# A hybrid attention layer on one core: head outputs stored as two half-precision parts and transposed by DMA on the way back

## The chip, the core and the metric

One core of a Trainium2 chip runs one launch of the kernel. Its engines have queues of their own, worked off in program order: TensorE (PE in the profile) multiplies matrices and also transposes, by a product with the identity; VectorE (DVE) and ScalarE (ACT) work element by element; GpSimd (POOL) and SyncE (SP) issue most of the DMA transfers here. The metric is the device time of a launch in microseconds (us), the median of several runs.

## What is computed

A decoder layer with two kinds of attention over one projected input, 2048 positions, width 1024, 16 heads of 64 columns, all in single precision:

```python
h = rms_norm(x, g_pre[l]) * (1.0 + scale[:, None, :]) + shift[:, None, :]
proj = h @ w_in[l]
qa, ka, va, fa, za, qb, kb, vb, zb = jnp.split(proj, split_points, axis=-1)
oa = forgetting_attention(qa, ka, va, fa + b_fgate[l])      # 8 heads, causal, reshapes left out
oa = oa * jax.nn.silu(za)
qb, kb = rope(qb, positions), rope(kb, positions)
ob = sliding_window_sink_attention(qb, kb, vb, sinks[l])    # 8 heads, window 128
ob = ob * jax.nn.silu(zb)
y = jnp.concatenate([oa, ob], axis=-1) @ w_out[l]
x = x + gate[:, None, :] * rms_norm(y, g_post[l])
```

The heads' outputs `oa` and `ob` side by side are the array of 2048 x 1024 that this change is about. It is multiplied by the gate `silu(z)` and then by `w_out`.

## The kernel before

Large products are made from half-precision parts: each single-precision operand is scaled and split into a high part and the rest (low), and high x high, high x low and low x high are summed in PSUM. That is why most products come in threes.

The kernel has four stages in one hand-written order. First come the adaLN projection and the normalised input. Then the sliding-window heads (`Pair`, 32 of them: four pairs of heads by eight pairs of 128-row blocks), with input projections as filler for TensorE between their steps. Then the forgetting heads (`Step`): 8 heads of 20 steps, each step two blocks of 128 keys against a chunk `ci` of 512 queries, again with projections as filler. Head 7 is the last; in it the weights `w_out` are loaded and split (`w_out_load`, `w_out_split`), and from its ninth step on the output projection is the filler (`ofill`). After the last step the rest of the output projection runs alone; this is the tail.

The order is written out by helpers. `after(n, f)` puts `f` off by `n` calls of `tick()`; a step of a head calls `tick` twice, the tail once every two filler units (`tick2`). A unit of the output projection (`ounits`) is the product of one slice of 128 rows for half the output columns: three matmuls (line 1489). A tile of 128 positions has 16 units.

A head's output goes this way. In `Step.pv` (line 1310) the last block of a chunk ends with a division by the row sum on VectorE (line 1327) into a tile `ona` of 128 x 256, which SP stores to DRAM, `o_d[ci]`, at line 1328; 32 such stores. In `Pair.pv` the same is done at line 913, and POOL stores at line 915; 32 stores. Rows of `o_d` are positions, so for the output projection, which needs the columns on the partitions, each tile of 128 positions must be transposed.

That is done by the class `Out`, one object for each of 16 tiles:

- `load` (line 1398) has SP load the tile's 128 x 1024 of `o_d` (line 1402, 512 KB) and its gate values `z_d` (line 1404, 512 KB) into slots of the array `Ts[0]`, which heads of even number use for their queries and keys. There are two slots of each, by the tile's parity.
- `turn` (line 1406) has TensorE make eight transposes of 128 x 128 in single precision into two PSUM banks (line 1410). Put off by ticks follow: the product with the gate on VectorE, two operations that read the banks (`gate`, line 1419); squares on ScalarE (1423); a matmul with ones that sums them over the partitions and the scale from it (1427, helper lines 121 and 122); the high part on ScalarE (1437) and the low part on VectorE (1438). The tile `oz` with both is what the products read.
- `product` (line 1476) makes the 16 units. Its evacuation reads PSUM on VectorE (1498) and ScalarE (1499); after the second half `root` and `store` follow, with `x` loaded at 1486 and the result stored at 1519, both by SP.

The loads of tiles 0 and 1 stand in head 7 behind its steps 4 and 6, their turns behind steps 6 and 8; tile 0's load needs chunk 0 of all heads in `o_d`, head 7's too. Later tiles are loaded at the first unit of the tile two before (`oloads`), and a turn is a unit of its own, behind the third unit of the tile before (line 1531). SP works its queue in order, so that a DMA whose input isn't there keeps all later ones waiting; in that part of head 7 the queue holds stores of outputs, loads of tiles, rows of query limbs (`ext_rows`, line 1208) and loads of `w_out` (line 1378).

Of the kernel before, what the change touches and what calls it, by code (L numbers as in the profile page):

```python
# [18 lines left out]
P = 128  # L19
# [22 lines left out]
def hybrid_layer(  # L42
# [33 lines left out]
    o_d = [dram.tile([CH, D], F32, name=f"o_d{t}") for t in range(NCH)]  # L76
# [189 lines left out]
    def w_split(key):  # L266
        w_scale(key)
        w_high(key)
        w_low(key, 0, 1)

# [566 lines left out]
    class Pair:  # L837
# [62 lines left out]
        def pv(self):  # L900
            j, i = self.j, self.i
            po = ps_pv.tile([P, 4, 64], F32, tag="pv", name="pob")
            for e, (i_, k0, nk) in enumerate(self.blocks):
                for h in range(2):
                    for b in range(nk):
                        for n, (pp_, vv) in enumerate(((0, 0), (0, 1), (1, 0))):
                            PE.matmul(po[:, 2 * e + h, :], self.ptt[:, pp_, self.at[e] + h * nk + b, :],  # L907
                                      vb[:, k0 + b, self.g, 64 * vv:64 * vv + 64],
                                      start=(b == 0 and n == 0), stop=(b == nk - 1 and n == 2))

            def out_():
                on = onp.tile([P, 2, P], F32, tag="on", name="on")
                V.tensor_tensor(on[:].rearrange("p e (h d) -> p (e h) d", h=2), po[:],
                                self.rinv[:].unsqueeze(2).broadcast_to([P, 4, 64]), op=ALU.mult)
                G.dma_start(o_d[i // 4][(i % 4) * P:(i % 4 + 2) * P, (4 + j) * P:(5 + j) * P]
                            .rearrange("(e p) c -> p e c", p=P), on[:])

            after(1, out_)
# [357 lines left out]
    class Step:  # L1276
# [33 lines left out]
        def pv(self):  # L1310
# [12 lines left out]
            if self.last:  # L1323
# [4 lines left out]
                SP.dma_start(o_d[self.ci][:, hd * 64:(hd + 1) * 64].rearrange("(u p) d -> p u d", p=P), on[:])  # L1328
# [26 lines left out]
    def open_out():  # L1355
        nonlocal op_, stp
# [4 lines left out]
        stp = foxo.enter_context(tc.tile_pool(name="stpo", bufs=4, reuse_waits="tile"))  # L1361
        oio["w"] = wo.tile([P, 2, KT, D], F16, name="wohl")
# [7 lines left out]
    w_raw = {}  # L1370
# [21 lines left out]
    class Out:  # L1392
# [5 lines left out]
        def load(self):  # L1398
            t = self.t
            rows_ = slice(t * P, (t + 1) * P)  # L1400
            self.o = Ts[0][:, t % 2, :].bitcast(F32)
            SP.dma_start(self.o, o_d[t // 4][(t % 4) * P:(t % 4 + 1) * P, :])
            self.z = Ts[0][:, 2 + t % 2, :].bitcast(F32).rearrange("p (k n) -> p k n", k=KT)
            SP.dma_start(self.z, z_d[:, :, rows_].rearrange("k p n -> p k n"))

        def turn(self, lag):

            px = [bk[bank()][:].rearrange("p (k n) -> p k n", k=4) for _ in range(2)]
            for k in range(KT):
                PE.transpose(px[k // 4][:, k % 4, :], self.o[:, k * P:(k + 1) * P], ident[:])  # L1410
# [5 lines left out]
            def gate():  # L1416
                for h in range(2):
                    z = self.z[:, 4 * h:4 * h + 4, :]
                    V.tensor_tensor(z, px[h], z, op=ALU.mult)
# [103 lines left out]
    ounits, oloads = [], {}  # L1523
    for t, n in [(0, 0), (1, 0), (0, 1), (1, 1)] + [(t, n) for t in range(2, NB) for n in range(2)]:
        if n == 0 and t + 2 < NB:
            oloads[len(ounits)] = t + 2
        for q in range(KT):
            ounits.append(lambda t=t, n=n, q=q: outs[t].product(n, q))
            nxt = 2 if (t, n) == (0, 1) else t + 1 if n == 0 and 2 <= t < NB - 1 else None
            if q == 2 and nxt:  # L1530
                ounits.append(lambda nxt=nxt: outs[nxt].turn(4))
    opos = [0]
    N_IN = 4 * KT + 1

    def ofill(n, each=None):
        for _ in range(n):
            if opos[0] in oloads:
                outs[oloads[opos[0]]].load()
# [5 lines left out]
    with tc.manual_schedule():  # L1544
# [99 lines left out]
        fxs.close()  # L1644
        ofill(len(ounits) - opos[0], tick2)
        for _ in range(4):
            tick()

    foxo.close()
# [32 lines left out]
```

## Time and profile before

| | us |
|---|---|
| runs: median (lowest, highest) of 3 | 1190.21 (1186.89, 1191.7) |
| span of the profiled execution | 1188.7 |
| TensorE matmuls busy | 1147.3 |
| VectorE busy | 914.1 |
| ScalarE busy | 665.9 |
| heads of forgetting attention end, tail begins | 1022.7 |
| last 48 matmuls begin | 1175.7 |

For the profiled execution the page gives its span, from the first to the last instruction, and no time beside it; the span lies 1.5 us under the median of the runs. Where the profile of a window is shown below, times are counted from the start of the span. In a timeline a row is the start, the duration, the engine, the line and the operation with the tile written and those read, `x` a count of instructions merged into the row, and in brackets the idle time before it with the instruction that ended it. In a table of groups the figures behind the bar are busy time in us and mean ns of one; behind the second bar stands the engine's idle time in front of them. TensorE's matmuls are pipelined, so a row of several lasts longer than the distance to the next one. `SPq` is the SP queue's issue of a DMA, not the transfer.

### The profile page before, as it was taken

The page shows a single profiled execution, that of the slowest core. Times are in us where ns is not written, and L with a number is a line of the kernel's source. Part 1 is how long each engine was busy: PE and PEld are TensorE (multiplying, and loading weights), DVE is VectorE, ACT ScalarE, POOL GpSimd, SP SyncE. Part 2 cuts the span into 40 slices and gives each one's busy share as a digit, 9 for nine tenths or more (in the row PEclk, how much of TensorE's full clock was granted, in tenths as well). Part 3 has the DMA queues.
Part 4 walks back from the last instruction along what each step waited for, and adds up shares of the span by engine and source line. Part 5 has one row for each costly group of instructions (what it writes and reads, how often), then busy time and mean ns, then how long its engine had stood idle before and what let it go on. Part 6 is the DMA issues. An engine that isn't in the chain of part 4 may idle for free.

```text
span 1188.7 us, 27244 instructions
## 1 busy us (share of the span) xinstructions
PE 1147.3 (97%) x10853; PEld 693.6 (58%) x10853; DVE 914.1 (77%) x2263; ACT 665.9 (56%) x1102; POOL 115.2 (10%) x231
## 2 busy tenths in 40 slices
PE   5899999999999998999999999999999999999997
PEld 2475556765558976555555555555555555555554
DVE  7876678687776748688888889887888887766665
ACT  2784345464655521476766667666666778433332
POOL 2000112212121211001000101001000000000000
PEclk9899999999999999999999999999999999999999
DMA  9745433314223322413325322212311345455642
GB/s 333 277 121 87 84 89 99 61 59 109 83 70 88 58 63 63 65 50 95 68 70 72 102 63 60 50 48 71 48 42 39 92 127 176 147 171 184 198 167 96
DMA packets 87579, 120.22 MB, mean 101 GB/s; under 512 B 27508, under 2 KB 63388, under 8 KB 87452
## 3 DMA queue, kind: packets, MB, share of 16 engines
q1 hardware_dynamic: 76184, 85.69, 24.4%
q0 software_dynamic: 10832, 32.50, 13.2%
q8 instruction: 85, 1.39, 0.6%
q14 instruction: 42, 0.34, 0.1%
q10 hardware_dynamic: 436, 0.28, 0.1%
HBM read 71.04 MB, written 25.18 MB: 81 GB/s over the span
## 4 chain that ended last, share of the span: by engine, by line
PE 79%; DVE 10%; DMA 6%; issue 2%; ACT 2%; SPq 1%; DVEq 0%; ACTq 0%
PE bk L317 29%; PE bk L1489 13%; PE bk L335 7%; PE sta L1295 4%; PE sta L1294 4%; PE bk L1245 4%; PE poa L1320 2%; PE poa L1321 2%; PE poa L1318 2%; DMA wa<-in_w_ada_dram 2%; PE pxb L888 2%; PE pss L855 2%; PE pob L907 2%; DVE a_m L1248 1%; PE bk L1410 1%
## 5 line engine op out<-in xcount | busy, mean ns | idle before, releaser
L1301 ACT ACTIVATE p<-sta,lift,scl_qk 128x1024 f32<-128x1024 f32 (+2 forms) x160 | 172.0, 1075 | 143.7 <-PE sta L1295 88.2
L317 PE MATMUL bk<-hT,wh_qk 128*128 128x512 f16 x768 | 195.3, 380 | 0.0
L1248 DVE TENSOR_REDUCE a_m<-bk 128x1 f32<-128x512 f32 x192 | 130.5, 686 | 55.2 <-PE bk L1245 54.0
L1308 DVE TENSOR_TENSOR pha<-p,pha 128x1024 f16<-128x1024 f32 (+2 forms) x160 | 169.1, 1057 | 0.2 <-ACT pha L1305 0.2
L1489 PE MATMUL bk<-wohl,oz 128*128 128x512 f16 x744 | 167.0, 379 | 0.7 <-DVE oz L1438 0.7
L1305 ACT ACTIVATE pha<-p 128x1024 f16<-128x1024 f32 (+2 forms) x160 | 148.1, 926 | 5.4 <-PE poa L1321 0.7
L1489 PEld LDWEIGHTS <-oz 128*128 128x128 f16 x744 | 71.9, 99 | 79.4 <-DVE oz L1438 2.8
L317 PEld LDWEIGHTS <-wh_qk 128*128 128x128 f16 x768 | 72.5, 98 | 78.2 <-issue 6.6
L1321 PE MATMUL poa<-vt,pha 128*128 128x65 f16 x1088 | 116.1, 192 | 1.4 <-DVE pha L1308 1.2
L1318 PE MATMUL poa<-vt,pha 128*128 128x65 f16 x1088 | 116.5, 193 | 0.5 <-DVE ona L1327 0.4
L1320 PE MATMUL poa<-vt,pha 128*128 128x64 f16 x1088 | 116.5, 194 | 0.0
L1245 PE MATMUL bk<-T 66*128 66x512 f16 (+2 forms) x320 | 110.2, 350 | 3.1 <-DVE a_m L1248 3.0
L1294 PE MATMUL sta<-T 128*128 128x512 f16 (+1 forms) x320 | 110.9, 346 | 2.5 <-ACT p L1301 2.4
L1318 PEld LDWEIGHTS <-pha 128*128 128x128 f16 x1088 | 101.5, 96 | 15.1 <-DVE ona L1327 1.5
L1295 PE MATMUL sta<-T 69*128 69x512 f16 (+1 forms) x320 | 109.8, 348 | 0.0
L1320 PEld LDWEIGHTS <-pha 128*128 128x128 f16 x1088 | 100.9, 97 | 11.4
L1321 PEld LDWEIGHTS <-pha 128*128 128x128 f16 x1088 | 100.8, 99 | 1.8 <-DVE pha L1308 1.7
L317 PE MATMUL bk<-hT,wh_za 128*128 128x512 f16 x384 | 99.7, 378 | 0.0
L335 PE MATMUL bk<-wh_va,hT 128*128 128x128 f16 x1536 | 90.7, 219 | 0.0
L335 PEld LDWEIGHTS <-hT 128*128 128x128 f16 x1536 | 87.5, 98 | 4.7 <-issue 2.1
L317 PE MATMUL bk<-hT,wh_zb 128*128 128x512 f16 x384 | 88.9, 379 | 0.0
L317 PE MATMUL bk<-hT,wh_qb 128*128 128x512 f16 x384 | 87.4, 379 | 0.0
(498 smaller groups left out, 1860.4 us busy)
## 6 DMA issues: line engine op xcount, KB each, us to landing
hT<-in_x_dram SPq DMA_DIRECT2D x20, 512.0 KB
wa<-in_w_ada_dram SPq DMA_DIRECT2D x16, 512.0 KB
z_d<-tz POOLq DMA_DIRECT2D x32, 256.0 KB, 2.9
T<-stq SPq DMA_DIRECT2D x64, 128.0 KB
T<-o_d SPq DMA_DIRECT2D x16, 512.0 KB
T<-z_d SPq DMA_DIRECT2D x16, 512.0 KB
out_dram<-hT SPq DMA_DIRECT2D x15, 512.0 KB
xt<-in_x_dram SPq DMA_DIRECT2D x12, 512.0 KB
```

Source lines behind the costliest of these rows:

```text
L317: PE.matmul(ps, whl[:, a, k, :], hT[ci][:, b, k, :], start=(k == 0 and n == 0), stop=(k == KT - 1 and n == 2))
L335: PE.matmul(ps[:, u * P:(u + 1) * P], hT[ci][:, a, k, u * P:(u + 1) * P], whl[:, b, k, :], start=(k == 0 and n == 0), stop=(k == KT - 1 an ...
L1245: PE.matmul(mx[:, :w], T[0:XM, 0, i * P:(i + 1) * P], T[0:XM, 2, pc * CH:pc * CH + w], start=True, stop=True)
L1294: PE.matmul(self.st[:, o:o + w], T[:, 3, kb_], T[:, 1, qc], start=True, stop=False)
L1295: PE.matmul(self.st[:, o:o + w], T[0:XR, 2, kb_], T[0:XR, 0, qc], start=False, stop=not diag)
L1301: A.activation(self.p32[:, :self.w], self.st[:, :self.w], AF.Exp, scale=scl[f"qk{self.hd}"][:], bias=lift[:])
L1305: A.activation(self.ph[:, 0, :self.w], self.p32[:, :self.w], AF.Copy)
L1308: V.tensor_tensor(self.ph[:, 1, :self.w], self.p32[:, :self.w], self.ph[:, 0, :self.w], op=ALU.subtract)
L1318: PE.matmul(po[:, u, :], ph[:, 0, pq], vt[:, b, hd, 0:65], start=(self.first and n == 0 and u == 0), stop=False)
L1320: PE.matmul(po[:, u, 0:64], ph[:, 0, pq], vt[:, b, hd, 65:VW], start=False, stop=False)
L1321: PE.matmul(po[:, u, :], ph[:, 1, pq], vt[:, b, hd, 0:65], start=False, stop=(self.last and n == len(self.blocks) - 1))
L1489: PE.matmul(py, self.hl[:, i, k, :], w_slot(8 * j + k)[:, cc], start=(k == 0 and m_ == 0), stop=(k == KT - 1 and m_ == 2))
```

## The change

The array `o_d` holds two half-precision parts for each element in place of one single-precision number. A new helper, `o_store`, makes the high part on ScalarE and the low part on VectorE and issues two stores, one for each part; it stands in for the store in both attentions, by one or two ticks later than before. `Out.load` issues two transposing DMAs in place of the plain one, so that the parts arrive with columns on the partitions. TensorE's eight transposes are gone, and `gate` adds the two parts on VectorE into a new tile `of` before the product with the gate.

The loads move. Slots become five: two as before in `Ts[0]`, and three in a new pool `ozp`, which is opened when the probabilities' pools of the heads are closed. Tiles 2 and 3 are loaded at units 0 and 8, the others 60 units ahead of their first unit, though not before unit 32, where the tail begins. A turn no longer counts as a unit and comes 22 units ahead of its tile's first unit (14 for tile 2); its scale follows five ticks behind, before it was four. The room for DMA descriptors of the POOL queue is halved to 8192 bytes a partition.

```diff
--- before.py
+++ after.py
@@ -73,7 +73,7 @@
     const = ctx.enter_context(tc.tile_pool(name="const", bufs=1))
     small = ctx.enter_context(tc.tile_pool(name="small", bufs=4))
 
-    o_d = [dram.tile([CH, D], F32, name=f"o_d{t}") for t in range(NCH)]
+    o_d = [dram.tile([2, CH, D], F16, name=f"o_d{t}") for t in range(NCH)]
     z_d = dram.tile([KT, P, S], F32, name="z_d")
     mx_d = [dram.tile([P, 1], F32, name=f"mx_d{n}") for n in range(3)]
 
@@ -267,6 +267,18 @@
         w_scale(key)
         w_high(key)
         w_low(key, 0, 1)
+
+    def o_store(on, pool, ci, rows_, cols_, eng, lag):
+
+        oh = pool.tile([P, 2] + list(on.shape)[1:], F16, tag="oh", name="oh")
+
+        def low():
+            V.tensor_tensor(oh[:, 1], on, oh[:, 0], op=ALU.subtract)
+            for n in range(2):
+                eng.dma_start(o_d[ci][n, rows_, cols_].rearrange("(u p) c -> p u c", p=P), oh[:, n])
+
+        after(lag, lambda: A.activation(oh[:, 0], on, AF.Copy))
+        after(lag + 1, low)
 
     pws = {}
     scl, isc, czs, kaps = {}, {}, {}, {}
@@ -912,8 +924,7 @@
                 on = onp.tile([P, 2, P], F32, tag="on", name="on")
                 V.tensor_tensor(on[:].rearrange("p e (h d) -> p (e h) d", h=2), po[:],
                                 self.rinv[:].unsqueeze(2).broadcast_to([P, 4, 64]), op=ALU.mult)
-                G.dma_start(o_d[i // 4][(i % 4) * P:(i % 4 + 2) * P, (4 + j) * P:(5 + j) * P]
-                            .rearrange("(e p) c -> p e c", p=P), on[:])
+                o_store(on[:], onp, i // 4, slice((i % 4) * P, (i % 4 + 2) * P), slice((4 + j) * P, (5 + j) * P), G, 1)
 
             after(1, out_)
 
@@ -1325,7 +1336,7 @@
                 V.reciprocal(rinv[:], po[:, :, 64])
                 on = op_.tile([P, 4, 64], F32, tag="ona", name="ona")
                 V.tensor_tensor(on[:], po[:, :, 0:64], rinv[:].unsqueeze(2).broadcast_to([P, 4, 64]), op=ALU.mult)
-                SP.dma_start(o_d[self.ci][:, hd * 64:(hd + 1) * 64].rearrange("(u p) d -> p u d", p=P), on[:])
+                o_store(on[:], op_, self.ci, slice(0, CH), slice(hd * 64, (hd + 1) * 64), SP, 1 if hd == 7 else 2)
 
         po_ = {}
 
@@ -1353,12 +1364,13 @@
         return oio["w"][:, n // KT, n % KT, :]
 
     def open_out():
-        nonlocal op_, stp
+        nonlocal op_, stp, osm
         foxl.close()
         hpx.close()
         wo = foxo.enter_context(tc.tile_pool(name="wo", bufs=1, reuse_waits="tile"))
         op_ = foxo.enter_context(tc.tile_pool(name="opo", bufs=2, reuse_waits="tile"))
         stp = foxo.enter_context(tc.tile_pool(name="stpo", bufs=4, reuse_waits="tile"))
+        osm = foxo.enter_context(tc.tile_pool(name="osm", bufs=1, reuse_waits="tile"))
         oio["w"] = wo.tile([P, 2, KT, D], F16, name="wohl")
 
         fm = sm(1, "w_p2")
@@ -1367,7 +1379,7 @@
         V.tensor_tensor(ysc[:], wrt[:], fm[:], op=ALU.mult)
         V.tensor_scalar(wsc[:], fac8[:], ysc[:], None, op0=ALU.mult)
 
-    w_raw = {}
+    w_raw, osm, ozp = {}, None, None
 
     def w_out_load(m):
         k, cc = m % KT, slice((m // KT) * CH, (m // KT + 1) * CH)
@@ -1398,25 +1410,29 @@
         def load(self):
             t = self.t
             rows_ = slice(t * P, (t + 1) * P)
-            self.o = Ts[0][:, t % 2, :].bitcast(F32)
-            SP.dma_start(self.o, o_d[t // 4][(t % 4) * P:(t % 4 + 1) * P, :])
-            self.z = Ts[0][:, 2 + t % 2, :].bitcast(F32).rearrange("p (k n) -> p k n", k=KT)
+            n = t % 2 if t < 4 else (t - 2) % 5
+            if n < 2:
+                o, z = Ts[0][:, n, :], Ts[0][:, 2 + n, :]
+            else:
+                v = ozp.tile([P, 2, 2, D], F16, tag="oz", name="ozt")
+                o, z = v[:, 0].rearrange("p a n -> p (a n)"), v[:, 1].rearrange("p a n -> p (a n)")
+            self.oT = o.rearrange("p (l k n) -> p l k n", l=2, k=KT)
+            for n in range(2):
+                SP.dma_start_transpose(self.oT[:, n], o_d[t // 4][n, (t % 4) * P:(t % 4 + 1) * P, :])
+            self.z = z.bitcast(F32).rearrange("p (k n) -> p k n", k=KT)
             SP.dma_start(self.z, z_d[:, :, rows_].rearrange("k p n -> p k n"))
 
         def turn(self, lag):
 
-            px = [bk[bank()][:].rearrange("p (k n) -> p k n", k=4) for _ in range(2)]
-            for k in range(KT):
-                PE.transpose(px[k // 4][:, k % 4, :], self.o[:, k * P:(k + 1) * P], ident[:])
             self.hl = wpool.tile([P, 2, KT, P], F16, tag=("whl", "wraw")[self.t % 2], name="oz")
             self.sc = sm(1, "w_pw")
             hi, lo = self.hl[:, 0], self.hl[:, 1]
             gs = sm(1, "w_mx")
 
             def gate():
-                for h in range(2):
-                    z = self.z[:, 4 * h:4 * h + 4, :]
-                    V.tensor_tensor(z, px[h], z, op=ALU.mult)
+                of = osm.tile([P, KT, P], F32, tag="of", name="of")
+                V.tensor_tensor(of[:], self.oT[:, 0], self.oT[:, 1], op=ALU.add)
+                V.tensor_tensor(self.z, of[:], self.z, op=ALU.mult)
 
             def squares_():
                 junk = stp.tile([P, KT, P], BF16, tag="st", name="zj")
@@ -1520,22 +1536,21 @@
 
     outs = [Out(t) for t in range(NB)]
 
-    ounits, oloads = [], {}
+    ounits, oev, start_ = [], {}, {}
     for t, n in [(0, 0), (1, 0), (0, 1), (1, 1)] + [(t, n) for t in range(2, NB) for n in range(2)]:
-        if n == 0 and t + 2 < NB:
-            oloads[len(ounits)] = t + 2
+        start_.setdefault(t, len(ounits))
         for q in range(KT):
             ounits.append(lambda t=t, n=n, q=q: outs[t].product(n, q))
-            nxt = 2 if (t, n) == (0, 1) else t + 1 if n == 0 and 2 <= t < NB - 1 else None
-            if q == 2 and nxt:
-                ounits.append(lambda nxt=nxt: outs[nxt].turn(4))
+    N_IN = 4 * KT
+    for t in range(2, NB):
+        oev.setdefault(KT * (t - 2) if t < 4 else max(N_IN, start_[t] - 60), []).append(outs[t].load)
+        oev.setdefault(start_[t] - (14 if t == 2 else 22), []).append(lambda t=t: outs[t].turn(5))
     opos = [0]
-    N_IN = 4 * KT + 1
 
     def ofill(n, each=None):
         for _ in range(n):
-            if opos[0] in oloads:
-                outs[oloads[opos[0]]].load()
+            for f in oev.pop(opos[0], []):
+                f()
             ounits[opos[0]]()
             opos[0] += 1
             if each:
@@ -1642,10 +1657,13 @@
         tick()
         tick()
         fxs.close()
+        ozx = ExitStack()
+        ozp = ozx.enter_context(tc.tile_pool(name="ozp", bufs=3, side="right", reuse_waits="tile"))
         ofill(len(ounits) - opos[0], tick2)
         for _ in range(4):
             tick()
 
+    ozx.close()
     foxo.close()
     fox.close()
     bkx.close()
@@ -1663,7 +1681,7 @@
     from concourse import mybir as _mybir
     from concourse.bass_utils import run_bass_kernel_spmd as _run
 
-    nc = _bacc.Bacc("TRN2", target_bir_lowering=False, num_devices=1)
+    nc = _bacc.Bacc("TRN2", target_bir_lowering=False, num_devices=1, dynamic_dma_scratch_size=8192)
     arrays, args = {}, []
     for name in _INS:
         a = _np.ascontiguousarray(inputs[name])
```

## The prediction, made before the run

> **What bounds the kernel now.** I read the page's shares and its chain first, then windows of each stage, then timelines of TensorE (PE), ScalarE (ACT), VectorE (DVE) and the SP queue round the outputs.
>
> ```profile
> span 1188.7 us, 27244 instructions
> PE 1147.3 (97%) x10853; PEld 693.6 (58%) x10853; DVE 914.1 (77%) x2263; ACT 665.9 (56%) x1102; POOL 115.2 (10%) x231
> PE 79%; DVE 10%; DMA 6%; issue 2%; ACT 2%; SPq 1%; DVEq 0%; ACTq 0%
> ...
> 200.00:300.00 100.00, 100.00 (x1114) 67.21 (x1112) 72.28 (x206) 54.23 (x152) 21.82 (x51) 1.00 0.33 81
> 600.00:700.00 100.00, 98.67 (x1022) 56.97 (x1018) 87.17 (x184) 65.36 (x75) 9.39 (x14) 1.00 0.36 73
> 940.00:960.00 20.00, 17.33 (x231) 11.03 (x230) 19.86 (x36) 17.05 (x23) 0.00 (x0) 1.00 0.23 68
> 1050.00:1100.00 50.00, 50.00 (x256) 25.52 (x255) 33.05 (x97) 16.30 (x31) 0.00 (x0) 1.00 0.53 176
> ```
>
> Window columns after the length: busy us of PE, weight loads, DVE, ACT, POOL, then granted clock, DMA share, GB/s. PE is full in the sliding-window stage (200 to 300), in the forgetting attention (600 to 700) and in the output projection (1050 on), at full clock. So what leaves PE there shortens the run, and work added to DVE or ACT there is covered, with little room at 87%. One stretch differs: from 940 to 960 DVE is busy for 19.86 of 20 us and PE stands for 2.7. That is head 7, where splitting the output weights comes on top.
>
> **What is removed.** The eight TensorE transposes of each output tile. The tail on PE, one tile from one turn to the next:
>
> ```profile
> 1058.80 1.04 PE L1410 MATMUL bk<-ident,T 128*128 128x128 f32 x8
> 1059.67 4.70 PE L1489 MATMUL bk<-wohl,oz 128*128 128x512 f16 x21
> 1064.20 0.28 PE L1427 MATMUL bk<-w_mx,ones 128*128 128x1 f32 x2
> 1064.34 5.99 PE L1489 MATMUL bk<-wohl,oz 128*128 128x512 f16 x27
> 1070.17 1.04 PE L1410 MATMUL bk<-ident,T 128*128 128x128 f32 x8
> ```
>
> The period is 1070.17 - 1058.80 = 11.37 us, and the transposes hold PE from 1058.80 to 1059.67: 0.87 us; the rest is 10.50. There are 16 tiles. Thirteen turns (tiles 3 to 15) lie in the tail; those of tiles 0 to 2 lie in head 7. The chain tells which of these are on the path:
>
> ```profile
> 976.01 0.45 PE bk L1410 x4
> 976.49 0.47 DVE T L1419
> 977.10 0.69 DVE T L1419
> 977.81 0.65 ACT zj L1423
> ...
> 1005.05 0.87 PE bk L1410 x8
> ```
>
> Tile 2's turn is on it whole, of tile 0's only 0.45 us: from 976 to 993 the path runs through DVE and ACT. So removed: 14 x 0.87 + 0.45 = **12.6 us**, against 16 x 0.87 = 13.9 if all counted.
>
> **What is added on the engines.** Each of the 64 stores (32 per attention) gets an ACT copy and a DVE subtraction of 128x256; each tile gets an addition of 128x1024, and its gating product is one 128x1024 from SBUF instead of two 128x512 from PSUM.
>
> ```profile
> L1419 DVE TENSOR_TENSOR T<-bk,T 128x512 f32<-128x512 f32 x32 | 20.6, 686 | 21.6 <-PE bk L1410 21.6
> L1308 DVE TENSOR_TENSOR pha<-p,pha 128x1024 f16<-128x1024 f32 x18 | 21.9, 1215 | 0.2 <-ACT pha L1305 0.2
> L1308 DVE TENSOR_TENSOR pha<-p,pha 128x384 f16<-128x384 f32 x6 | 3.3, 550 | 0.0
> L1305 ACT ACTIVATE pha<-p 128x1024 f16<-128x1024 f32 x18 | 18.9, 1051 | 0.2
> L1305 ACT ACTIVATE pha<-p 128x384 f16<-128x384 f32 x6 | 3.1, 516 | 0.2
> ```
>
> On a straight line through the two sizes, 256 columns take 0.550 - 128 x 0.00104 = 0.42 us on DVE and 0.516 - 128 x 0.00084 = 0.41 on ACT. The joining costs DVE 2 x 1.215 - 2 x 0.686 = +1.06 us per tile; in the tail DVE goes from 33.05 / 50 x 11.37 = 7.5 us to 8.6 of 10.5. That stays hidden behind PE: 0. If PE's cover were gone it would be 16 x 1.06 = 17 us. On the path it counts for tiles 0 and 1: **+2.1**. Two of the stores fall where ACT and DVE are the path (943 and 980): 2 x 0.4 = **+0.8**. The other 62 are covered by PE; uncovered they would cost 62 x 0.42 = 26. PE's waits of the attention stages were small, and I add **+0.5** for them.
>
> The turn of tile 3 moves out of the tail into the last two steps of head 7, and with it its DVE work (2.4 for joining, then the low part):
>
> ```profile
> 1022.52 0.20 PE L1321 MATMUL poa<-vt,pha 128*128 128x65 f16 x1 [0.61 <-DVE pha L1308]
> 1022.74 2.11 PE L1489 MATMUL bk<-wohl,oz 128*128 128x512 f16 x9
> ```
>
> PE already waits 0.61 us for DVE there, with the last softmax parts queued behind whatever DVE does first. Bounds 0 and 2.4; I take **+1.0**, the length of one of the two operations, roughly.
>
> **The moved wait.** Tile 0 can only be loaded when head 7's first output has landed. Before, one DVE result went straight to the store:
>
> ```profile
> 967.47 0.42 DVE L1327 TENSOR_TENSOR ona<-poa,a_ri 128x256 f32<-128x256 f32 x1
> ...
> 970.42 0.68 DVE L357 SCALAR_TENSOR_TENSOR tz<-tz,bk 128x512 f32<-128x512 f32 x1
> ...
> 976.49 1.29 DVE L1419 TENSOR_TENSOR T<-bk,T 128x512 f32<-128x512 f32 x2 [2.03 <-PE bk L1410]
> ```
>
> ```profile
> 967.92 0.38 SPq L1328 DMA_DIRECT2D o_d<-ona  x1
> 969.97 0.33 SPq L1402 DMA_DIRECT2D T<-o_d  x1
> 970.51 0.37 SPq L1404 DMA_DIRECT2D T<-z_d  x1
> 971.28 0.67 SPq L1208 DMA_DIRECT2D T<-rw  x1
> 972.05 0.34 SPq L1378 DMA_DIRECT2D hT<-in_w_out_dram  x1
> ```
>
> Now the ACT copy and the subtraction come first, the latter by the order of the code beside line 357's operation, ending near 971; two store issues of 0.4 and the 2.05 us from store to load (967.92 to 969.97) bring the load to about 973.7, 3.7 us later. Behind it on SP wait tile 0's gate rows, a row of query limbs and weight loads, all needed several us later. The gating on DVE stands next in order at 974.4 and already waited 2.03 us for PE. With 0.7 for the issues, 2.05 to land and 1.56 (below) it starts near 978 instead of 976.49: by that count +1.5, less overlap of landing and transfer: **+1.2**. Behind it on DVE stand the subtractions for the probabilities, and PE waits for those. Lower bound 0 (the old wait hides it); the upper one is the second rival.
>
> **The transposing loads.** The trace shows none. Per tile two of 256 KB replace one load of 512 KB:
>
> ```profile
> q1 hardware_dynamic: 12235, 18.19, 54.8%
> ...
> T<-o_d SPq DMA_DIRECT2D x9, 512.0 KB
> ```
>
> ```profile
> q1 hardware_dynamic: 17976, 9.47, 13.9%
> ```
>
> ```profile
> q1 hardware_dynamic: 76184, 85.69, 24.4%
> ```
>
> The first fence is the queues between 1050 and 1150: 54.8% of an 11.37 us period is 6.23 us of all 16 engines per tile for four transfers of 512 KB, so 1.56 each and 4.67 without the outputs. Lower bound for the pair: 1.56, as a plain load. For small pieces: between 550 and 850 (second fence) a packet, of 527 B on the mean, took 0.139 x 16 x 300 / 17976 = 37 ns; over the whole run (third fence) 0.244 x 16 x 1188.7 / 76184 = 61 ns. Were the pair 2 x 128 x 8 = 2048 pieces of 256 B, it would take 2048 x 37 / 16 = 4.7 us, or 7.8 at 61 ns. Tile time on DMA: 6.2, 9.4 or 12.5 us against PE's 10.5. I take a value between the first two, as both rows nearest in size lie below 10.5: hidden, **0**. Prefetch of nearly four tiles covers latency but not rate.
>
> [...]
>
> Sum: -12.6 + 2.1 + 0.8 + 0.5 + 1.0 + 1.2 = **-7.0**: the profiled span of 1188.7 becomes 1181.7. The median, 1190.2, lies 1.5 above that span, so I forecast **1183 us**.
>
> **Rivals.** (1) *The transposes set the tail's pace.* At 12.5 us of DMA per tile the loads of tiles 4 to 15, which start with the tail, take 150 us. The tail starts near 1022.7 + 4.3 = 1027 (the sum without the 13 tail turns: -7.0 + 11.3), so the last lands at 1177; joining, squares, scale and split take some 6.8; and from the last tile's first matmul to the end it was 18.1 us:
>
> ```profile
> 1166.03 9.87 PE L1489 MATMUL bk<-wohl,oz 128*128 128x512 f16 x45
> 1175.74 5.40 PE L1453 MATMUL bk<-wohl,oz 128*128 128x256 f16 x48
> ```
>
> (1175.74 - 24 x 0.216 = 1170.6, and 1188.7 - 1170.6.) End 1202, time **1203**. It decides from a pair of (1027 + 13 x 10.5 - 6.8 - 1027) / 12 - 4.67 = 6.1 us, and the kernel is slower than before from (1170.6 - 6.8 - 1027) / 12 - 4.67 = 6.7. The same holds if SP is held that long by the issue. For it: small pieces, and a share of DMA time that already reads 0.53. Against: the 37 ns row.
>
> (2) *Head 7 eats the gain.* With a pair at 4.7 to 7.8 the first gating stands 3.1 to 6.2 us longer, DVE with it and PE behind: 1186 to 1189, say **1188**. For it: the path there runs through DVE and ACT already. Against: the wait comes once, and tile 1's load follows at once.
>
> (3) *The 28 stores of heads 0 to 6 aren't hidden*, DVE being the bound at 87%: 28 x 0.42 = 11.8, so **1195**. Against: PE is full in that window.
>
> **Chances.** Forecast 0.54, first rival 0.19, second 0.22, third 0.05. What a measurement of this kernel tells from no change is 0.5%, 6 us: faster means below 1184.3. The forecast's own range is 1178 to 1187, and 0.45 of its 0.54 lies below 1184.3, with 0.05 of the second rival; same is the other 0.09 and 0.17 of that rival; slower is the first and the third. The range, 1177 (head 7 costs almost nothing) to 1201, leaves out some 0.05 below and the dearer half of the first rival above.
>
> **What would show it.** No PE work of 0.87 us between tiles and a period of 10.5 in the tail: the removal. PE waiting for the gated tiles, with DMA share near 1: the first rival. DVE standing for a transposing load near 975, and for how long: the moved wait. DVE's idle time in the heads gone and PE below 98%: the third. Wrong would be a period above 10.5 with idle DMA, or a tail that starts more than 6 us later.

## The result, and the profile after

The changed kernel takes **1201.85 us** (median; 1199.08 to 1204.9) against 1189.26 (1186.89 to 1191.7) for the kernel before on the same chip: 1.0104 times as long, interval 1.0078 to 1.013, or 12.6 us more. The forecast was 1183, with a range of 1177 to 1201. The execution profiled took 1203.64, with a span of 1201.9, 13.2 more than the span before. In the changed kernel the store's subtraction is line 276, its transfers 278, the transposing load 1421, the load of the gate rows 1423, the joining addition 1434, the gate product 1435, and the scale's small product 1443. The page's head and its chain:

```profile
span 1201.9 us, 27313 instructions
PE 1143.9 (95%) x10725; PEld 682.9 (57%) x10725; DVE 950.8 (79%) x2327; ACT 684.0 (57%) x1166; POOL 137.7 (11%) x263
...
PE 70%; DVE 13%; DMA 7%; issue 4%; ACT 3%; SPq 1%; POOL 0%; DVEq 0%; ACTq 0%; POOLq 0%
```

PE's work fell by only 3.4 us, although 128 of its instructions are gone (a slower clock gave part of it back: 2.7 us on 48 matmuls, below), while the span grew by 13.2: PE now stands for 16.6 us more. In the chain PE has gone from 79% to 70%, and DVE, DMA and "issue" (waits for nothing that the profile shows) have grown.

To find where, I followed one instruction that both kernels have 64 times: the division on DVE that makes a head output. The last of the sliding-window stage, before and then after:

```profile
433.19 0.42 DVE L913 TENSOR_TENSOR on<-pob,b_ri 128x256 f32<-128x256 f32 x1 [4.66 <-PE pob L907]
```

```profile
437.26 0.42 DVE L925 TENSOR_TENSOR on<-pob,b_ri 128x256 f32<-128x256 f32 x1 [4.66 <-PE pob L919]
```

It comes 4.07 us later after the change. Head 7's first output (967.47 before) comes 6.3 us later, its second 9.9, and its last 15.1. From there on the run gains only 2, where 11.3 were forecast. So the time is lost in the sliding-window stage (4.1), between it and head 7's first output (2.2), between head 7's first two outputs (3.6), in head 7's last steps (most of another 5.2) and in the tail, which gives 9.4 less than forecast. In four of these places TensorE stands. Windows of after there (columns as in the prediction):

```profile
374.00:378.00 4.00, 2.35 (x40) 2.10 (x38) 1.69 (x4) 1.54 (x8) 1.67 (x3) 1.00 0.69 108
...
985.00:990.00 5.00, 0.59 (x2) 0.53 (x3) 3.25 (x7) 2.27 (x4) 0.00 (x0) 0.82 1.13 228
990.00:995.00 5.00, 4.82 (x32) 2.29 (x32) 4.44 (x7) 5.00 (x7) 0.54 (x1) 0.50 0.69 186
...
1030.00:1035.00 5.00, 3.25 (x38) 1.83 (x36) 4.69 (x13) 2.48 (x5) 0.00 (x0) 1.00 0.00 0
1035.00:1040.00 5.00, 3.67 (x36) 2.66 (x37) 4.23 (x9) 1.19 (x3) 0.00 (x0) 0.66 0.00 0
...
1060.00:1065.00 5.00, 3.26 (x16) 1.27 (x13) 3.16 (x3) 0.78 (x2) 0.00 (x0) 1.00 1.12 213
1065.00:1070.00 5.00, 2.44 (x7) 1.16 (x8) 3.43 (x14) 2.96 (x5) 0.00 (x0) 0.67 1.07 287
1070.00:1075.00 5.00, 5.00 (x16) 1.91 (x15) 3.68 (x8) 0.78 (x2) 0.00 (x0) 0.65 1.02 288
```

Before, PE was full in each of these eight stretches; the first two:

```profile
374.00:378.00 4.00, 4.00 (x78) 3.81 (x77) 1.25 (x3) 1.73 (x8) 0.91 (x2) 1.00 0.74 86
985.00:990.00 5.00, 5.00 (x74) 3.55 (x72) 4.39 (x10) 5.00 (x8) 0.00 (x0) 1.00 0.91 262
```

PE stands in each place, and in three of the four its granted clock reads 0.50 to 0.67 in the stretch behind, so that the work behind these three waits is slower too. The waits by name, from the view of waits between 366 and 410 (first row) and between 970 and 1080 (the others): engine, tile, line, what it waited for, us in total, times, longest.

```profile
PE bk L347 <- issue: 2.9, 3, 1.3
...
PE bk L1443 <- ACT zj L1439: 9.9, 4, 4.5
PE poa L1332 <- DVE pha L1319: 3.1, 1, 3.1
```

```profile
DVE hT L1514 <- DMA out_dram<-hT: 3.4, 1, 3.4
DVE of L1434 <- DMA T<-o_d: 3.0, 1, 3.0
DVE T L1435 <- DMA T<-z_d: 1.7, 1, 1.7
DVE hT L1534 <- DMA hT<-in_x_dram: 1.6, 1, 1.6
```

Behind the 9.9 us for which PE waits at line 1443, DVE stands for a transposing load and gate rows (head 7), and later for an output store and a load of x: transfers that share SP's queue and the DMA engines with the loads of tiles 4 to 7 (a DMA share of 1.02 to 1.12 in the last three windows). Head 7's part, in time:

```profile
973.77 0.42 DVE L1338 TENSOR_TENSOR ona<-poa,a_ri 128x256 f32<-128x256 f32 x1
...
976.71 0.42 DVE L276 TENSOR_TENSOR oh<-ona,oh 128x256 f16<-128x256 f32 x1
...
983.55 1.22 DVE L1434 TENSOR_TENSOR of<-T 128x1024 f32<-128x1024 f16 x1 [3.04 <-DMA T<-o_d]
986.47 1.22 DVE L1435 TENSOR_TENSOR T<-of,T 128x1024 f32<-128x1024 f32 x1 [1.69 <-DMA T<-z_d]
```

```profile
977.76 2.92 SPq L1421 DMA_TRANSPOSE T<-o_d  x2
980.86 0.47 SPq L1423 DMA_DIRECT2D T<-z_d  x1
```

Issuing the two transposing loads holds SP for 2.92 us, and the gate rows behind them arrive later than the output itself. The start of the tail on SP's queue, and the operation on DVE that waits for it:

```profile
1041.94 2.60 SPq L1421 DMA_TRANSPOSE ozt<-o_d  x2
...
1046.27 3.50 SPq L1421 DMA_TRANSPOSE ozt<-o_d  x2
...
1050.44 3.80 SPq L1421 DMA_TRANSPOSE ozt<-o_d  x2
...
1054.96 0.52 SPq L1535 DMA_DIRECT2D out_dram<-hT  x1
...
1056.01 6.30 SPq L1421 DMA_TRANSPOSE T<-o_d  x2
```

```profile
1060.27 0.75 DVE L1514 SCALAR_TENSOR_TENSOR hT<-bk,w_sw,gacc 128x512 f32<-128x512 f32 x1 [3.40 <-DMA out_dram<-hT]
```

The loads of tiles 4, 5 and 6 follow each other almost without a gap, and tile 7's comes soon after. The result that line 1535 stores was ready on DVE at 1046.03; its store is issued 8.9 us later, behind the loads of tiles 5 and 6, and DVE can reuse the buffer only when it has landed. The tail from there:

```profile
1067.57 0.58 PE L1443 MATMUL bk<-w_mx,ones 128*128 128x1 f32 x2 [4.31 <-ACT zj L1439]
1068.01 13.24 PE L1505 MATMUL bk<-wohl,oz 128*128 128x512 f16 x48
1081.09 0.28 PE L1443 MATMUL bk<-w_mx,ones 128*128 128x1 f32 x2
...
1091.58 0.28 PE L1443 MATMUL bk<-w_mx,ones 128*128 128x1 f32 x2
...
1102.08 0.28 PE L1443 MATMUL bk<-w_mx,ones 128*128 128x1 f32 x2
```

From 1081 a tile takes 10.50 us, as forecast. Ahead of that, behind a wait of 4.31, 48 matmuls took 13.24, where the 48 before that wait took 10.52.

### The profile page after: what moved, and what is told of

It is laid out like the page before. It is cut to its first block, busy times and chain, and to the rows that moved or that the text cites. A ratio compares the mean times of both kernels' runs of the same rounds, so it can differ in the third digit from the quotient of the medians.

```text
span 1201.9 us, 27313 instructions
## 1 busy us (share of the span) xinstructions
PE 1143.9 (95%) x10725; PEld 682.9 (57%) x10725; DVE 950.8 (79%) x2327; ACT 684.0 (57%) x1166; POOL 137.7 (11%) x263
## 4 chain that ended last, share of the span: by engine, by line
PE 70%; DVE 13%; DMA 7%; issue 4%; ACT 3%; SPq 1%; POOL 0%; DVEq 0%; ACTq 0%; POOLq 0%
PE bk L329 26%; PE bk L1505 10%; PE bk L347 6%; PE bk L1256 4%; PE sta L1306 4%; PE sta L1305 4%; PE poa L1331 2%; PE poa L1332 2%; PE poa L1329 2%; DMA wa<-in_w_ada_dram 2%; PE pxb L900 2%; PE pss L867 2%; PE pob L919 1%; DVE a_m L1259 1%; DMA T<-stq 1%
## 5 line engine op out<-in xcount | busy, mean ns | idle before, releaser
L1332 PE MATMUL poa<-vt,pha 128*128 128x65 f16 x1088 | 117.3, 193 | 3.9 <-DVE pha L1319 3.9
L1329 PE MATMUL poa<-vt,pha 128*128 128x65 f16 x1088 | 117.9, 194 | 0.8 <-DVE ona L1338 0.7
```

The lines of the kernel that those rows point to most:

```text
L1329: PE.matmul(po[:, u, :], ph[:, 0, pq], vt[:, b, hd, 0:65], start=(self.first and n == 0 and u == 0), stop=False)
L1332: PE.matmul(po[:, u, :], ph[:, 1, pq], vt[:, b, hd, 0:65], start=False, stop=(self.last and n == len(self.blocks) - 1))
```

## The experiments

Each time stands beside the kernel before on the same chip (1189.19 to 1189.82 in the four groups). The theory after the result: four separate losses, by the stores, by tile 3's early turn, by the burst of loads as the tail starts, and by the late load of tile 0. The rivals were the arithmetic of the split, the transposition itself, and the smaller descriptor room. The diffs are shortened, some indices to words.

**Plain loads instead of transposing ones.**

```diff
-                SP.dma_start_transpose(self.oT[:, n], o_d[t // 4][n, rows of tile t])
+                SP.dma_start(the same buffer's half n, o_d[t // 4][n, rows of tile t])
```

> The changed kernel with two plain loads of 256 KB in place of the two transposing ones; it leaves out the transposition, so the tiles hold rows where columns are wanted. Theory (order and waits, not the transposing itself, lose the time): the heads up to head 7 are as late as in the changed kernel (about 6 us), the 3 us wait of PE for the last softmax part before the tail stays, and the time is 1192 to 1199. Rival (the slow transposing transfer loses it): the standing of VectorE near 982 and the waits of 4 us in the tail go, and the time is 1182 to 1188.

Measured: 1194.26, ratio 1.0041 (1.0026 to 1.0056). So transposing itself is worth 7.6 us of the changed kernel, and even with plain loads the change is slower than before. PE is then full from 1045 to 1150; head 7 keeps its waits (DVE stood 2.2 us for tile 0's load, PE 3.1 at the last low parts).

**The loads of tiles 4 to 15 spread out.**

```diff
-        oev.setdefault(... max(N_IN, start_[t] - 60), []).append(outs[t].load)
+        oev.setdefault(... max(N_IN, start_[t] - 44), []).append(outs[t].load)
```

> The changed kernel with the loads of tiles 4 to 15 44 units ahead instead of 60, so that no four of them are issued together at the start of the tail. Theory (the burst of four tiles' loads delays the stores and the x loads in the same queue, VectorE stands for them, and PE follows): the waits of 4 us between 1050 and 1070 and the low clock behind them go, 6 to 8 us, time 1193 to 1196. Rival (tile 4 is simply late, by the place of its load): the waits stay, 1200 to 1203.

Measured: 1196.4, ratio 1.0053 (1.0036 to 1.007), 5.4 us less than the changed kernel and 0.4 above what the theory gave. The execution profiled was its slowest, 1201.6: it lost more in head 7 and before. Its tail doesn't show that; the windows there:

```profile
1065.00:1075.00 10.00, 10.00 (x50) 4.68 (x48) 7.93 (x22) 3.74 (x7) 0.00 (x0) 1.00 1.06 289
1075.00:1150.00 75.00, 75.00 (x359) 35.15 (x358) 60.44 (x149) 26.20 (x49) 0.00 (x0) 1.00 0.71 202
```

PE is full where it stood in the changed kernel, at full clock and about the same DMA share. The rate of the transposing loads was no limit; issuing three to four tiles' loads in a row was.

**The stores alone**, on the kernel before.

```diff
-                SP.dma_start(o_d[self.ci][:, cols].rearrange("(u p) d -> p u d", p=P), on[:])
+                o_store(on[:], op_, self.ci, slice(0, CH), cols, SP, 1 if hd == 7 else 2)
...
-            SP.dma_start(self.o, o_d[t // 4][rows of tile t])
+            for n in range(2):
+                SP.dma_start(half n of the same buffer, o_d[t // 4][n, rows of tile t])
```

> The kernel before with the new stores alone (two half-precision parts split on ScalarE and VectorE, descriptor room halved), plain loads and TensorE's transposes as before; it leaves out joining the parts, which are read as if they were single-precision numbers. Theory (the stores and their splitting cost 6 us before head 7's first output and a little more in head 7): 1195 to 1198. Rival (the 6 us come from something else in the changed kernel's front): 1189 to 1191.

Measured: 1201.48, ratio 1.0098 (1.0078 to 1.0118): the stores alone cost 11.7 us, more than the theory had. That is nearly the net loss of 12.6; with the 12.6 that the removed transposes should give, there are some 25 us to explain. The 11.7 hold head 7's late load of tile 0 too, for this run also waits there for both parts.

**The descriptor room alone** (the change halves it; nothing else is edited).

> The kernel before with the descriptor room of the POOL queue halved and nothing else. Theory (more transfers and packets of the stores hold up the fetching of instructions where PE's are densest, not the room): 1188 to 1191, no loss between 370 and 410. Rival (the smaller room does it): 1193 to 1196 with the steps of 2 and 1.5 us there.

Measured: 1189.8, ratio 1.0002 (0.9992 to 1.0011). Not a cause.

**The arithmetic of the split alone.**

```diff
                 SP.dma_start(o_d[self.ci][...], on[:])
+                o_split(on[:], op_, 1 if hd == 7 else 2)     # ACT copy, DVE subtraction, no store
```

> The kernel before with its single-precision stores, its loads and TensorE's transposes; beside each of the 64 stores ScalarE and VectorE also make the two half-precision parts, which are stored nowhere. Also the descriptor room of the changed kernel. The split stores alone cost 11.7 us (1201.48 against 1189.73). Theory that it is the two engines' work (0.3 to 0.5 us on each for a store, in stages where they end last): 1198 to 1202, with the outputs late as in that run (3.8 us by head 7's first output, 6.7 by its second). Rival, that it is the transfers (twice the descriptors, packets of half the size, the parts leaving two slots later): 1189 to 1192, and no wait of the matmuls called issue near 375 and 405 us.

Measured: 1192.62, ratio 1.0028 (1.0015 to 1.0041), so 3.2 us (1.8 to 4.9), between the two. Most of the stores' cost isn't the engines' work. The outputs were at most 0.8 us late.

**One transfer a store instead of two**, the rest as in the stores alone.

```diff
-            for n in range(2):
-                eng.dma_start(o_d[ci][n, rows_, cols_].rearrange("(u p) c -> p u c", p=P), oh[:, n])
+            eng.dma_start(o_d[ci][2 * u0:2 * u1, :, cols_].rearrange("m p c -> p m c"), oh)
```

> The split stores on the kernel before, as in the run of the stores alone, but both parts of an output leave in one transfer (the scratch tensor is laid out so that the row blocks of both parts follow each other): 64 transfers instead of 128, the same packets and bytes, the same arithmetic; the joining is left out here too. If the number of transfers and of their issues costs the time: 1191 to 1196. If it is the arithmetic, or the packets, it stays at 1199 to 1203.

Measured: 1198.84, ratio 1.0071 (1.0052 to 1.0091): 2.6 us less than with two, at the edge of what the intervals tell apart, and outside both expectations. In its profile the last sliding-window output still comes 4.4 us late.

**Tile 3's turn back in the tail.**

```diff
-        oev.setdefault(start_[t] - (14 if t == 2 else 22), []).append(...turn(5))
+        oev.setdefault(start_[t] - (14 if t == 2 else 16 if t == 3 else 22), []).append(...turn(5))
```

> The changed kernel with tile 3's turn begun 16 units ahead of its product instead of 22, so inside the tail and no longer among head 7's last steps. Theory that this turn's five DVE instructions are what holds head 7's last matmuls (3.07 us of waiting at 1036 us, then a granted clock of 0.66 for 5 us): 1196 to 1199.5, the wait of L1332 under 1.5 us. Rival, that VectorE is late there anyway from the wait for tile 0's load: 1200 to 1203.

Measured: 1197.16, ratio 1.0059 (1.0039 to 1.008), 4.7 us less than the changed kernel. Its windows there:

```profile
1030.00:1035.00 5.00, 4.01 (x60) 2.51 (x57) 4.34 (x10) 1.20 (x3) 0.00 (x0) 1.00 0.00 0
1035.00:1040.00 5.00, 4.95 (x23) 2.06 (x21) 4.65 (x15) 0.00 (x0) 0.00 (x0) 1.00 0.71 182
```

The wait for the last low parts fell from 3.1 us to 0.7 at most, and the clock stayed at 1.00 where it had been 0.66. The burst of loads is still in this run, and PE stands in its tail as well.

**Only the forgetting heads split**, on the stores alone; the sliding-window columns are kept in single precision.

```diff
-                o_store(on[:], onp, i // 4, rows, cols, G, 1)
+                G.dma_start(o_s[i // 4][rows, cols].rearrange("(e p) c -> p e c", p=P), on[:])
```

> As the run of the stores alone, but only the 32 outputs of the forgetting heads are split; the 32 of the sliding-window heads are stored as before, by one single-precision transfer from POOL's queue. The joining is left out here too. The arithmetic of all 64 cost 3.2 us (1192.62), all of the stores 11.7 (1201.48). Theory that the sliding-window stage pays most of the difference (its outputs are 4 to 7.5 us late by 433 us in every profile with split stores there, with matmul waits called issue, and not in the three without) and head 7's late load the rest, 3 us: 1193 to 1196. Rival, that the later stages pay it: 1198 to 1201.

Measured: 1194.54, ratio 1.0048 (1.0032 to 1.0064). So the 32 sliding-window stores cost 7 of the 11.7 us. In this profile no PE wait between 366 and 440 is called issue, and the stage's last output comes 0.9 us late. For head 7 there remain a wait of DVE of 5.0 us for tile 0's gate rows and these waits of PE between 970 and 1045 (the load and its follower):

```profile
PE bk L1442 <- ACT zj L1438: 1.4, 1, 1.4
...
PE bk L1425 <- DMA T<-o_s: 0.6, 1, 0.6
PE bk L1425 <- DMA T<-o_d: 0.3, 1, 0.3
```

**The sliding-window stores from SP's queue**, on the stores alone.

```diff
-                o_store(on[:], onp, i // 4, rows, cols, G, 1)
+                o_store(on[:], onp, i // 4, rows, cols, SP, 1)
```

> As the run of the stores alone, with the sliding-window heads' split stores issued from SP's queue instead of POOL's; the number of transfers, packets, bytes and the arithmetic stay, and the joining is left out as there. Those stores cost 7 us of the 11.7 (1201.48 with them, 1194.54 without). If what is late is what stands behind them in POOL's queue (the weights' column maxima and weight loads): 1194 to 1197, outputs at 433 us at most 1 us later than before, the waits called issue under 1 us. If it is the 2,048 more packets of the stage themselves, on the 16 DMA engines: 1199 to 1203 and the same 4 us late at 433.

Measured: 1197.21, ratio 1.0063 (1.0046 to 1.0079): 4.3 of the 7 us are gone, with the same packets; the time is 0.2 above what the queue theory gave, and the outputs at 433 are 2.1 late where it gave 1. The profiles say it more clearly than the times. From the output at 368 us to the next, in which PE's standing near 376 falls, the eight profiles with split sliding-window stores on POOL's queue take 0.5 to 5.8 us longer than before, those with one transfer a store among them; none of the six others does, of which three have these stores on SP's queue. What stands behind those stores on POOL, in the changed kernel (first fence) and before (second):

```profile
367.71 1.42 POOL L278 DMA_DIRECT2D o_d<-oh  x2
...
376.33 0.55 POOL L229 DMA_DIRECT2D mxr<-mx_d  x1 [6.00 <-issue]
```

```profile
374.35 0.58 POOL L229 DMA_DIRECT2D mxr<-mx_d  x1 [4.17 <-DMA mx_d<-w_mx]
```

A weight's column maxima are written to DRAM and read back by the same queue; the reading starts 2 us later, of which 0.6 is the lateness of what stands before it. PE's standing at the same time falls in the middle of a sum, the profile names nothing that it waits for, and in some executions it is longer: four profiles of the same instructions up to head 7 had 0.5, 2.9, 3.3 and 3.3 us of it between 366 and 440. What PE waits for there isn't shown by any run. The fetching of instructions, named in the theory of the run with the smaller descriptor room, finds no support: between 373.5 and 379.5 the changed kernel's profile has no transfer on the queues for instructions. Nor do the runs tell the order in POOL's queue from POOL's dearer issue (0.71 us a store, against a median of 0.38 for SP's), as moving the stores changes both.

**A version with chunk 0 in single precision.** Tiles 0 to 3 go as before, with TensorE's transposes; the others are split with one transfer a store, and their loads begin 44 units ahead.

```diff
+            if t < 4:
+                SP.dma_start(self.o, o_d0[rows of tile t])          # and PE.transpose in turn()
+            else:
                 for n in range(2):
-                    SP.dma_start_transpose(self.oT[:, n], o_d[t // 4][n, rows of tile t])
+                    SP.dma_start_transpose(self.oT[:, n], o_d[t // 4][2 * (t % 4) + n])
```

> A version meant to be better than both: chunk 0 (tiles 0 to 3) goes as before, in single precision and with TensorE's transposes at their old places; chunks 1 to 3 in two parts by one transfer a store, their loads transposed and begun 44 units ahead, none with a turn in head 7. 12 tiles lose 0.87 us each, 10.4 in all; against it stand three quarters of what the stores cost before head 7 (3.8 us in the run of the stores alone), 3 us, and up to 2 in head 7. Expected 1181 to 1187. Rival, that the split stores cost their 11 us wherever they are made: 1188 to 1193.

Measured: 1186.53, ratio 0.997 (0.9958 to 0.9982): by 0.3% faster than the kernel before, and inside what was expected, near its upper end. Three variants of it follow. The sliding-window stores from SP's queue:

```diff
-                    o_store(on[:], onp, i // 4, rows, cols, G, 1)
+                    o_store(on[:], onp, i // 4, rows, cols, SP, 1)
```

> The version with chunk 0 in single precision, with the split stores of the sliding-window heads issued from SP's queue instead of POOL's; bytes, packets and arithmetic the same. If POOL's queue (the column-maximum round trips of the weights and the weight loads stand in it) is what makes the sliding-window stage late: 1182.5 to 1185 against 1186.53, outputs at 433 us not over 1 us later than before. Rival, that it is the packets themselves, from whatever queue: 1185.5 to 1188, and still 2 us late at 433.

Measured: 1184.64, ratio 0.9966 (0.9948 to 0.9984), and the outputs at 433 are 0.2 us early where the version itself has them 2.1 late; as the queue theory had it, though the ratios of the two versions can't be told apart.

Tile 4's turn later:

```diff
-            oev.setdefault(start_[t] - 22, []).append(lambda t=t: outs[t].turn(5))
+            oev.setdefault(start_[t] - (16 if t == 4 else 22), []).append(lambda t=t: outs[t].turn(5))
```

> The version with chunk 0 in single precision, with tile 4's turn begun 16 units ahead of its product instead of 22, so that VectorE isn't held for tile 4's load (1.2 us at 1040) while tile 3's parts are due (2.0 us of waiting by L1527's matmuls). Theory: 1184 to 1186 against 1186.53. Rival, that tile 4's own turn is then too late and its first product waits instead: 1186 to 1189.

Measured: 1184.86, ratio 0.9958 (0.9944 to 0.9972), inside the theory's bounds. But the profile has the rival's wait as well: PE waits 1.28 us at 1049 for tile 4's low parts, where tile 3's had been late, so the gain isn't shown to come from this edit.

Both, and tile 3's turn earlier:

```diff
+            if (t, n, q) == (2, 0, 0):
+                ounits.append(lambda: outs[3].turn(4))
             ounits.append(lambda t=t, n=n, q=q: outs[t].product(n, q))
-            nxt = {(0, 1): 2, (2, 0): 3}.get((t, n))
-            if q == 2 and nxt:
-                ounits.append(lambda nxt=nxt: outs[nxt].turn(4))
+            if (t, n, q) == (0, 1, 2):
+                ounits.append(lambda: outs[2].turn(4))
```

> The version with chunk 0 in single precision, with three edits together: sliding-window stores from SP's queue (1184.64 alone), tile 4's turn 16 units ahead of its product (1184.86 alone), and tile 3's turn ahead of tile 2's first product instead of behind its third, since the 2.0 us for which the matmuls of L1527 wait at 1035 to 1042 us are tile 3's parts. If the edits add: 1180.5 to 1183.5. Rival, that SP's queue and the later turn don't add: 1183.5 to 1186.5.

Measured: 1185.56, ratio 0.9969 (0.9956 to 0.9982): the edits don't add.

```profile
1032.34 0.38 PE L1465 MATMUL bk<-w_mx,ones 128*128 128x1 f32 x2 [1.26 <-ACT zj L1461]
...
1050.78 1.68 PE L1527 MATMUL bk<-wohl,oz 128*128 128x512 f16 x7 [1.28 <-DVE oz L1476]
```

Tile 3's turn is now too early (its squares aren't ready for line 1465) and tile 4's too late. The three variants can't be told apart, nor from the version that they vary, and each is 0.3 to 0.4% faster than before.

**Three stretches in the profiles.** From head 7's first output to its second, from its third to its last, and from the last to the end of the span, in us; the profiles beside each other separate what the times mix:

| | first to second | third to last | tail |
|---|---|---|---|
| before | 11.57 | 22.70 | 165.5 |
| changed kernel | 15.19 | 27.29 | 163.6 |
| plain loads | 13.97 | 27.10 | 156.2 |
| loads spread out | 16.69 | 27.27 | 156.0 |
| stores alone | 14.39 | 22.78 | 166.1 |
| arithmetic alone | 11.29 | 22.78 | 165.9 |
| tile 3's turn back | 16.00 | 24.70 | 159.5 |
| chunk 0 in single precision | 11.29 | 22.79 | 157.0 |

The first stretch is longer wherever tile 0 comes from the two-part stores, with plain loads too, and not by the arithmetic. The second is longer where tile 3's turn is early; 2.6 of its 4.6 us go with the turn, and what the other 2.0 are isn't shown. In the tail the spread-out loads give 9.5 us against before, nearly the 11.3 forecast, and plain loads no more.

## Why the prediction was wrong, step by step

**The transposes removed, -12.6: right.** The period of 10.50 us is there from 1081 on.

**The transposing loads at 0: right as a rate, wrong as a burst.** SP's queue is busy for 70.5% between 1090 and 1150:

```profile
q1 hardware_dynamic: 20255, 12.00, 70.5%
```

The figure is the time of the packets as a share of 16 engines' time: 7.40 us of the 10.50. Without the 4.67 of a tile's other transfers, if they cost what they did before, a pair takes an estimated 2.7, between the bounds of 1.56 and 4.7 as chosen. With plain loads the same stretch reads 57.5%, 1.4 us less for a tile. So the first rival is out: the transposes don't set the tail's pace, and that its 1203 lies near the measured time is coincidence. But the step said that prefetch of nearly four tiles covers latency, and did not price its start. The loads of tiles 4 to 7 stand in a row in one queue with output stores and loads of x, at a DMA share of 1.07 from 1045 to 1075, and each holds the queue for 2.6 to 6.3 us. Spreading them out gave 5.4 us, all of the transposition 7.6.

**The 62 covered stores at +0.5 and the two others at +0.8: the step that failed.** I priced ACT's and DVE's work, which measured 3.2 in all, and not the transfers; the stores cost 11.7, some 3 of them in head 7, by the table's first column. Twice the transfers on POOL's queue, in a stage where PE was full, were taken as covered because the engine work was. 7 us are the sliding-window stage's, of which 4.3 go with the queue. The third rival (11.8 us in heads 0 to 6) is refuted in its size: in the changed kernel's profile only 0.9 us are lost from head 1's first output (5.04 late) to head 6's last (5.96).

**Tile 3's turn at +1.0, bounds 0 and 2.4: mis-sized.** It measured 4.7 as a difference of two medians; in the profiles 2.6 of it lie before the last output. The bounds held only two DVE operations. The addition and product (1030.75 to 1033.2) also stood behind a low part that waits 1.74 us for ACT, and ahead of the root's chain of small operations; PE's 3.1 us of waiting was then followed by a clock of 0.66.

**The moved wait at +1.2: right for the output, wrong for the gate rows.** From head 7's first output to the end of tile 0's gate product it took 977.79 - 967.47 = 10.3 us before and 987.69 - 973.77 = 13.9 after: 3.6 more, where 1.2 for the wait and 1.06 for joining were forecast. The addition waited for the load as forecast: it begins 9.78 us after that output, where the gating began after 9.02, so 0.8 later. But the step had the gate rows among what is "needed several us later"; they are needed as soon as the addition ends, and they came 1.69 us later still. Their issue behind the 2.92 us of the transposing loads doesn't explain it: with plain loads DVE stood 1.3 us for them. Here the second rival is partly right: DVE and PE do stand in head 7, but for a different transfer in part.

**The joining at +2.1** wasn't measured alone.

The sum by the two profiles, with the forecast terms of the same stretch in brackets: +6.3 up to head 7's first output (+0.9: the waits and half of the +0.8), +3.6 up to its second (+1.8: the moved wait and one joining, less tile 0's 0.45), +5.2 up to its last (+1.6: the other additions, less tile 2's 0.87), -1.9 in the tail (-11.3); +13.2 in all, against -7.0. The runs don't part all of it, and since differences of two medians are uncertain by 2 to 3 us, the effects of single edits needn't add up to it. The prediction named a tail that starts over 6 us later as what would make it wrong; it started 15 us later.

## What to carry to other kernels

Price the transfers of an edit as well as its engine work, on the queue they stand in, and name what is queued behind them there: here the stores in two parts cost 11.7 us and their arithmetic 3.2. A prefetch that covers a rate must also be started gently; here three tiles' loads in a row held up the very stores and loads that free the next buffers, one store by 8.9 us. Work moved across the end of a stage is to be costed with all that stands before and behind it on its engine, and a wait on TensorE with the slower clock behind it: here one of 4.31 us, and 2.7 us more on the 48 matmuls that followed.

## What the runs showed of the hardware

**TensorE's granted clock read half behind three of its waits, for 3.4 to 6.8 us.** The kernel before ran at a granted clock of 1.00 in all the stretches shown above. After the change it reads 0.50 from 990 to 995, behind a wait of 4.51 us; 0.66 from 1035, behind one of 3.07; and 0.67 and 0.65 from 1065 to 1075, round the end of one of 4.31. By the microsecond these are stretches of exactly half clock between stretches of full clock:

```profile
1066.00:1067.00 1.00, 0.00 (x0) 0.00 (x0) 0.93 (x2) 0.64 (x1) 0.00 (x0) 0.85 0.89 185
1067.00:1068.00 1.00, 0.43 (x2) 0.44 (x3) 0.00 (x0) 1.00 (x4) 0.00 (x0) 0.50 0.86 300
...
1073.00:1074.00 1.00, 1.00 (x5) 0.40 (x4) 0.67 (x2) 0.00 (x0) 0.00 (x0) 0.73 1.16 385
1074.00:1075.00 1.00, 1.00 (x6) 0.46 (x5) 1.00 (x2) 0.78 (x2) 0.00 (x0) 1.00 0.84 328
```

The clock was halved for 6.8 us here (0.3 of the first row, six whole rows, 0.5 of the fourth), for 6.8 round 990 and for 3.4 behind the wait of 3.07. The price here was 2.7 us on 48 matmuls (13.24 against 10.52). In all three it fell while TensorE still stood: some 3.8 us into the wait of 4.51, 2.7 into that of 3.07 and 3.4 into that of 4.31. One wait's length doesn't settle it: waits of 0.36 and 1.29 us near 376 left the changed kernel's clock at 1.00, while in the kernel before waits of 1.26 and 1.57, which ended at 472.75 and 475.19, were followed by 3.4 us at half. It also differs between executions of much the same work. Between the two attention stages, from 470 to 490, the clock reads 0.91 before, 1.00 with the smaller descriptor room and 0.83 in the version with chunk 0 in single precision, and from the last sliding-window output to the first forgetting one it takes 67.78, 65.70 and 69.96 us. So one profile's lateness can't be read finer than some 2 us across that place.

**Issuing a transposing transfer held SP's queue longer than issuing a plain one.** In head 7 one took SP 1.26 to 3.80 us (median 1.68 of eight), against 0.47 to 0.59 for the gate rows' plain load beside it, and 0.33 to 0.54 for the plain loads of the same parts in the first experiment:

```profile
L1421 SPq DMA_TRANSPOSE T<-o_d x8: 1261/1679/3802, 977.8 to 1000.0; - x8
L1423 SPq DMA_DIRECT2D T<-z_d x4: 466/520/587, 980.9 to 1003.9; - x4
```

By the estimate above the pair moved 512 KB in 2.7 us, some 192 GB/s.
